# Attention outputs in one fp32 piece, returns on GpSimd's queue, and another order of filler and finishing in a fused attention layer

## The chip, the cores and the metric

The kernel runs on one core of a Trainium2 chip. The metric is the device time of one launch in microseconds (us). The time before is the median of three runs. One further execution was recorded by the hardware profiler; all rows of a profile are from that execution.

## The reference

One decoder layer on 512 tokens of width 2048, in fp32: native sparse attention with 16 heads of 128 in 4 groups, then a SwiGLU feed-forward block, RMS norms before both and at the end. Cut to what matters here:

```python
hn = rmsnorm(x, mix_norm_g)
q, kc, vc, ks, vs, kw, vw, gl = split(hn @ w_in)        # 16 q heads; 4 groups of keys and values
p_c = masked_softmax(q @ kcc + bias_c)                  # compressed branch: 31 blocks per group
p_s = masked_softmax(q @ ks + bias)                     # selected branch: 16 blocks wanted, 8 exist, so all
p_w = masked_softmax(q @ kw + bias)                     # window of 512: all tokens before
o   = g0 * (p_c @ vcc) + g1 * (p_s @ vs) + g2 * (p_w @ vw)   # per head, gates g = sigmoid(gl)
h   = x + o.reshape(S, 2048) @ w_out
out = rmsnorm(h + (silu(a) * b) @ ffn_w_out, final_norm_g)   # a, b = rmsnorm(h) @ ffn_w_in
```

## The kernel before

fp32 products are made of three TensorE matmuls. Each operand is split into a high part of a shorter type (fp32r), made by a copy on ScalarE, and a low part, made by a subtraction on VectorE; `three()` (L266 to 269) adds high x high, high x low and low x high. Weights arrive by DMA as `raw` in pieces of 128x1024, and `Weights.split` makes `whi` (ScalarE, L97) and `wlo` (VectorE, L98) of each, some pieces ahead of their use. In the attention stage the weights' loads go on GpSimd's queue. Each engine runs its instructions in the order in which the program emits them; a DMA that must wait also holds what stands behind it on its queue.

The attention stage lies at about 200 to 700 us of the profiled execution. Sixteen heads follow each other, each in twelve steps. For head h and step i the loop emits, in this order:

- `fetch(t)` (L812): the probabilities of the 128 tokens of tile t are read back from DRAM (`d_p`) into `ptr`, in another order. It is on SyncE's queue.
- `turn`: one piece of the probabilities is split into `pth` (ScalarE, L829) and `ptl` (VectorE, L833; the compressed branch's piece in L831). Steps 0 to 8.
- `scores(h+1, t)` at steps 2, 5, 8 and 11 for t = 3, 2, 1, 0: matmuls of q and k, then on VectorE a sum with the bias and its maximum (L791, `mx`), and on ScalarE the exponential (L793), into a buffer `P[t]`. Tiles 3 and 1 share one buffer, tiles 2 and 0 the other.
- `finish(h+1, t)` at steps 3, 6 and 9 for t = 3, 2, 1, and at step 0 of the head itself for t = 0: VectorE normalizes and gates the probabilities (L798 to 805) and turns them in blocks of 32x32 (L806); four DMAs on SyncE's queue write them to `d_p` (L808).
- `values`: the matmuls of probabilities and v (`o`), from step 2 on, two steps behind their `turn`. The last of a head, at step 10, is the compressed branch's (L844, with `vcc`). Then `head_out` (L849) splits the head's output: heads 12 to 15 straight into `hn_h` and `hn_l`, heads 0 to 11 into two tiles `of`, which two DMAs write to DRAM (`d_o`).
- `pump` (L735): filler from one long generator, `dense()`, whose granules are 3 matmuls of 512 columns or 6 of 256 and count 650 ns in the program's own accounts. The filler makes q of two heads, then the keys or the values of a group, in units of 32 granules (q, k, q, v, q, k, ...: thirteen units, the last one q of heads 14 and 15, written q14 below), and then four `partial` products of the output projection, of 24 granules each. `pump` emits until the accounts reach a goal that grows with head and step: four steps ahead, at 20,800 ns a head up to the thirteenth unit and 18,300 from there on. A q unit ends in an eviction: `yt` (VectorE, L319), `qh` (ScalarE, L292), `ql` (VectorE, L293).

`hn_h` and `hn_l` first hold the normed input that the filler multiplies. While q14 is emitted, the outputs of heads 0 to 11 come back from `d_o` into these tiles (`reload_o`, six DMAs of 1 MB on SyncE's queue, each after the matmuls that used that part). A partial product (L699) multiplies heads 0 to 11 with a quarter of the columns that it covers, adds x, which a DMA on SyncE's queue brings into `stage`, and a DMA on that queue writes the sum to `d_h`.

Ahead of the loop a prologue emits the scores (0,3) to (0,0) of head 0 with some filler behind each (`pump(-1, ...)`), and their `finish` and `fetch`. Behind the loop come the rest of the output projection and the feed-forward block, to the end of the span.

Of the kernel before, what the change touches and what calls it, by code (L numbers as in the profile page):

```python
# [10 lines left out]
F32 = mybir.dt.float32  # L11
F32R = mybir.dt.float32r
I32 = mybir.dt.int32
AF = mybir.ActivationFunctionType
OP = mybir.AluOpType
# [4 lines left out]
S, D, H, DH, G, HPG = 512, 2048, 16, 128, 4, 4  # L20
# [153 lines left out]
def nsa_block(ctx: ExitStack, tc: tile.TileContext, x, rel_bias, mix_g, ffn_g, fin_g, w_in, w_out,  # L174
              pos_k, w1k, w2k, pos_v, w1v, w2v, f_in, f_out, onehot, out):
    nc = tc.nc
    mm, act, dve, pool = nc.tensor.matmul, nc.scalar.activation, nc.vector, nc.gpsimd
# [6 lines left out]
    dram = ctx.enter_context(tc.tile_pool(name="dram", bufs=1, space=DRAM))  # L184
# [10 lines left out]
    hn_h, hn_l = hn_t = [hnp.tile([128, KC, S], F32R, name=f"hn_{x}") for x in "hl"]  # L195
    d_t = dram.tile([H, UL], F32, name="d_t")
    d_u = dram.tile([128, H * UL], F32, name="d_u")
    d_c = dram.tile([H, 16 * CL], F32, name="d_c")
    d_o = dram.tile([12, 2, 128, S], F32, name="d_o")
    d_h = dram.tile([S, 256 * N_SPILL], F32, name="d_h")  # L200
    d_r = dram.tile([NT, 128, D], F32, name="d_r")
    d_a = dram.tile([NF // 2, 128, 2 * S], F32, name="d_a")
# [87 lines left out]
    def split_from(psum_ap, hi, lo, scale=None):  # L290
        if scale is None:
            act(hi, psum_ap, AF.Copy)  # L292
            dve.tensor_tensor(lo, psum_ap, hi.bitcast(F32), op=OP.subtract)  # L293
        else:
            act(hi, psum_ap, AF.Copy, scale=scale)
            dve.scalar_tensor_tensor(lo, psum_ap, scale, hi.bitcast(F32), op0=OP.mult, op1=OP.subtract)
# [333 lines left out]
    with ExitStack() as st2:  # L630
# [24 lines left out]
        def qpair(h0):  # L655
            ps = proj2()
            end = q_out(ps, h0)
            for i in range(4):
                yield from ws(ps, i, W.take(), end=end)
                if h0 == H - 2 and i < 3:  # L660
                    reload_o(i)
            done["n"] += 1
            yield None

# [27 lines left out]
            yield None  # L692

        def reload_o(i):
            for part, t in enumerate((hn_h, hn_l)):
                nc.sync.dma_start(t[:, 4 * i:4 * i + 4].bitcast(F32),
                                  d_o[4 * i:4 * i + 4, part].rearrange("h p s -> p h s"))

        def partial(cb):  # L699
            st = stage_tile().rearrange("p (t c) -> p t c", t=NT)  # L700
            c = slice(256 * cb, 256 * (cb + 1))
            nc.sync.dma_start(st, x[:, c].rearrange("(t p) c -> p t c", p=128))
            ps = [p.rearrange("p (t c) -> p t c", t=2) for p in proj2()]
            for i in range(3):
                w = W.take()
                for t in range(NT):
                    if i == 2 and t == 2:
                        W.ahead(3)
                    for k in range(4):
                        h = 4 * i + k  # L710
                        three(ps[t // 2][:, t % 2], hn_h[:, h, tok(t)], hn_l[:, h, tok(t)], w[0][:, k], w[1][:, k],
                              h == 0 and t % 2 == 0, h == 11)
                        if k % 2:
                            yield 650
                    if i == 2 and t % 2:
                        b = t // 2
                        dve.tensor_tensor(st[:, 2 * b:2 * b + 2], st[:, 2 * b:2 * b + 2], ps[b], op=OP.add)
            nc.sync.dma_start(d_h[:, c].rearrange("(t p) c -> p t c", p=128), st)
            done["n"] += 1
            yield None  # L720

# [12 lines left out]
        STEPS = 12  # L734

        def pump(h, step):
            at = h + (step + 4) / STEPS
            goal = 20800 * min(at, 13) + 18300 * max(at - 13, 0)
            while done["ns"] < goal:
                c = next(stream, "end")  # L740
                if c == "end":
                    return
                done["ns"] += c or 0
# [66 lines left out]
        def fetch(t):  # L810

            nc.sync.dma_start(PT[:, :, PT_STEP * t:PT_STEP * t + runs[t]], d_p[t].rearrange("j a i r -> (j a) i r"))  # L812
# [6 lines left out]
        def turn(h, b, kt):  # L819
            n = S - 128 * kt  # L820
            th = ap_.tile([128, 512], F32R, name="pth", bufs=3)
            tl = ap_.tile([128, 512], F32R, name="ptl")
            rows = 128 if b >= 0 else 96
            if b < 0:
                src = arrived(rows, 64, 0, PT_STEP + 64)
            else:
                src = arrived(rows, PT_STEP * kt + 32 * (kt + 1) * b + 32 * kt, kt, PT_STEP + 32 * b)
            th4, tl4 = (x[:rows, :n].rearrange("p (t i s) -> p t i s", i=4, s=32) for x in (th, tl))
            act(th4, src, AF.Copy)  # L829
            if b < 0:  # L830
                dve.tensor_tensor(th4[32:64], src[32:64], th4[32:64].bitcast(F32), op=OP.subtract)  # L831
            else:
                dve.tensor_tensor(tl4, src, th4.bitcast(F32), op=OP.subtract)  # L833
            HS[h]["t", b, kt] = th[:rows, :n], tl[:rows, :n]
# [14 lines left out]
        def head_out(h):  # L849
            o = HS[h]["o"]  # L850
            if h < 12:
                f = [ap_.tile([128, S], F32R, name=f"of{i}", bufs=1) for i in range(2)]
                split_from(o, *f)
                for i in range(2):
                    nc.sync.dma_start(d_o[h, i], f[i].bitcast(F32))
            else:
                split_from(o, hn_h[:, h], hn_l[:, h])
            del HS[h]
# [2 lines left out]
        load_bias(0)  # L861
        load_bias(1)
        for i in range(4):
            scores(0, 3 - i)
            if i:
                finish(0, 4 - i)
            if i > 1:
                fetch(5 - i)
            pump(-1, min(9 + i, 11.7))
        for h in range(H):  # L870
            seq = [(b, kt) for kt in (3, 2, 1, 0) for b in (0, 1)] + [(-1, 0)]
            for i in range(STEPS):
                if i == 4:
                    load_bias(h + 2)
                if i in (0, 3):
                    fetch(1 - i // 3)
                if i < 9:
                    turn(h, *seq[i])
                if i == 8 and h + 1 < H:
                    fetch(3)  # L880
                    fetch(2)
                if i == 0:
                    finish(h, 0)
                if h + 1 < H:
                    if i == 2:
                        drain_to(needed(h + 1))
                    if i % 3 == 2:
                        scores(h + 1, 3 - i // 3)
                    elif i % 3 == 0 and i:
                        finish(h + 1, 4 - i // 3)  # L890
                if 2 <= i < 11:
                    if i == 2 and h % HPG == 0:
                        drain_to(h)
                    values(h, *seq[i - 2])
                    if i == 10:
                        head_out(h)
                pump(h, i)
        W.queue = nc.sync
# [591 lines left out]
```

## Time and profile before

| | |
|---|---|
| median of three runs | 2136.5 us (2135.11 to 2139.32) |
| the profiled execution | 2137.68 us, of which its span is 2136.0 us |
| attention stage | about 200 to 700 us |
| TensorE busy | 2103.2 us, 98% of the span |
| VectorE busy | 1634.8 us, 77% |
| ScalarE busy | 922.9 us, 43% |
| granted TensorE clock, mean | 0.996 |

In the profile PE is TensorE, PEld its weight load, DVE VectorE, ACT ScalarE, POOL GpSimd, SP SyncE, and SPq a DMA queue fed by SyncE. A row of a timeline gives start, duration, engine, line, operation, output and inputs, partitions and elements, and in brackets the engine's idle time before it and what ended it. A row of the busy times by stretch gives, for each engine, the busy us and the instructions in it, then the granted clock (PEclk), the busy share of the DMA engines and their GB/s. A row of the waits gives the engine and line that waited, what released it, the us in total, the times and the longest.

### The profile page before, as it was taken

The numbers are of one execution on the slowest core, as the hardware profiler recorded it, in microseconds if no ns is written. First come the engines' busy times: TensorE is split into PE (matmuls) and PEld (weight loads), VectorE is DVE, ScalarE is ACT, GpSimd is POOL, SyncE is SP. The second block draws the span as 40 slices with busy tenths as digits, with TensorE's granted clock in tenths as the row PEclk, the third lists the DMA queues.
The fourth block names the chain that finished last, engine by engine and source line by source line (L and its number), as shares of the span: only waits on it lengthen the run. The fifth ranks groups of instructions, "written<-read, shape, count | busy, mean of one in ns | idle before, by whom it ended". The sixth has DMA issues, their size and how long they took to land.

```text
span 2136.0 us, 37198 instructions
## 1 busy us (share of the span) xinstructions
PE 2103.2 (98%) x14697; PEld 1949.5 (91%) x14697; DVE 1634.8 (77%) x2680; ACT 922.9 (43%) x1433; POOL 118.2 (6%) x195
## 2 busy tenths in 40 slices
PE   9999999999998999999999999999999999999998
PEld 7898788898988889899999999999999888999996
DVE  5565777878776357898888888888888787877785
ACT  5344454555544234444444343443434444544344
POOL 1000111111100000000000000000000000001000
PEclk9999999999999999999999999999999999999999
DMA  7555777776787643344434344433344776878894
GB/s 226 174 158 149 195 203 202 194 209 197 207 295 211 218 137 111 118 130 128 129 126 122 122 126 129 129 119 125 123 129 129 256 278 220 299 268 308 307 336 143
DMA packets 279147, 394.37 MB, mean 185 GB/s; under 512 B 34763, under 2 KB 208891, under 8 KB 278332
## 3 DMA queue, kind: packets, MB, share of 16 engines
q1 hardware_dynamic: 255324, 289.68, 43.5%
q0 software_dynamic: 21744, 98.12, 13.3%
q10 hardware_dynamic: 1904, 4.20, 0.5%
q8 instruction: 115, 1.88, 0.4%
q14 instruction: 60, 0.49, 0.1%
HBM read 323.67 MB, written 73.50 MB: 186 GB/s over the span
## 4 chain that ended last, share of the span: by engine, by line
PE 87%; DVE 5%; DMA 4%; ACT 2%; issue 2%; SPq 1%; POOL 0%; ACTq 0%; DVEq 0%; POOLq 0%
PE f L268 19%; PE f L269 19%; PE f L267 19%; PE proj L267 7%; PE proj L268 6%; PE proj L269 6%; DMA d_p<-p 1%; DVE wlo L98 1%; DMA ptr<-d_p 1%; PE pp L269 1%; PE pp L268 1%; PE pp L267 1%; PE po L269 1%; PE po L267 1%; PE po L268 1%
## 5 line engine op out<-in xcount | busy, mean ns | idle before, releaser
L98 DVE TENSOR_TENSOR wlo<-raw,whi 128x1024 fp32r<-128x1024 f32 (+1 forms) x226 | 270.6, 1200 | 117.2 <-ACT whi L97 116.7
L97 ACT ACTIVATE whi<-raw 128x1024 fp32r<-128x1024 f32 (+1 forms) x226 | 234.4, 1040 | 230.4 <-DVE raw L989 124.7
L989 DVE TENSOR_TENSOR tlo<-tt,thi 128x1536 fp32r<-128x1536 f32 (+2 forms) x135 | 197.1, 1460 | 110.1 <-ACT thi L1091 89.1
L267 PE MATMUL f<-hn_h,whi 128*128 128x256 f32 x984 | 271.7, 276 | 0.8 <-ACT E L1049 0.8
L269 PE MATMUL f<-hn_h,wlo 128*128 128x256 f32 x984 | 271.6, 276 | 0.0
L268 PE MATMUL f<-hn_l,whi 128*128 128x256 f32 x984 | 271.6, 276 | 0.0
L1086 ACT ACTIVATE whi<-raw 128x1024 fp32r<-128x1024 f32 x123 | 126.1, 1057 | 292.2 <-DVE raw L989 281.9
L267 PE MATMUL proj<-hn_h,whi 128*128 128x512 f32 x512 | 204.1, 399 | 0.5 <-ACT hn_h L402 0.5
L268 PE MATMUL proj<-hn_l,whi 128*128 128x512 f32 x512 | 200.7, 392 | 0.3 <-DVE hn_l L403 0.3
L269 PE MATMUL proj<-hn_h,wlo 128*128 128x512 f32 x512 | 200.9, 392 | 0.0
L267 PEld LDWEIGHTS f<-hn_h,whi 128*128 128x128 f32 x984 | 184.7, 188 | 1.2 <-ACT E L1049 1.2
L269 PEld LDWEIGHTS f<-hn_h,wlo 128*128 128x128 f32 x984 | 184.7, 188 | 0.0
L268 PEld LDWEIGHTS f<-hn_l,whi 128*128 128x128 f32 x984 | 184.7, 188 | 0.0
L1091 ACT ACTIVATE thi<-tt 128x1536 fp32r<-128x1536 f32 x82 | 121.8, 1486 | 84.8 <-PE f L268 75.3
L989 DVE TENSOR_TENSOR wlo<-raw,whi 128x1024 fp32r<-128x1024 f32 x123 | 147.0, 1223 | 0.0
L267 PE MATMUL proj<-whi,hn_h 128*128 128x256 f32 (+2 forms) x496 | 146.7, 296 | 0.0
L269 PE MATMUL proj<-whi,hn_l 128*128 128x256 f32 (+2 forms) x496 | 146.0, 294 | 0.0
L268 PE MATMUL proj<-wlo,hn_h 128*128 128x256 f32 (+2 forms) x496 | 145.9, 294 | 0.0
L269 PE MATMUL f<-whi,tlo 128*128 128x512 f32 x320 | 124.9, 390 | 0.6 <-DVE tlo L989 0.6
L268 PE MATMUL f<-wlo,thi 128*128 128x512 f32 x320 | 125.0, 391 | 0.0
L267 PE MATMUL f<-whi,thi 128*128 128x512 f32 x320 | 124.7, 390 | 0.0
L269 PEld LDWEIGHTS proj<-hn_h,wlo 128*128 128x128 f32 x512 | 96.5, 189 | 21.5 <-DVE wlo L98 0.2
(323 smaller groups left out, 6087.1 us busy)
## 6 DMA issues: line engine op xcount, KB each, us to landing
raw<-in_ffn_w_in SPq DMA_DIRECT2D x135, 512.0 KB, 3.8
raw<-in_ffn_w_out SPq DMA_DIRECT2D x88, 512.0 KB, 5.7
rawx<-in_ffn_w_in SPq DMA_DIRECT2D x41, 512.0 KB, 4.8
rawx<-d_a SPq DMA_DIRECT2D x31, 512.0 KB, 5.2
ah<-d_s POOLq DMA_DIRECT2D x16, 896.0 KB, 7.0
al<-d_s POOLq DMA_DIRECT2D x16, 896.0 KB, 9.5
raw<-in_nsa_w_in SPq DMA_DIRECT2D x24, 512.0 KB, 5.1
raw<-in_nsa_w_in POOLq DMA_DIRECT2D x24, 512.0 KB, 4.7
```

Source lines behind the costliest of these rows:

```text
L97: self.nc.scalar.activation(hi[:, :n], src, AF.Copy)
L98: self.nc.vector.tensor_tensor(lo[:, :n], src, hi[:, :n].bitcast(F32), op=OP.subtract)
L267: mm(o, ah, bh, start=start, stop=False, skip_group_check=True)
L268: mm(o, ah, bl, start=False, stop=False, skip_group_check=True)
L269: mm(o, al, bh, start=False, stop=stop, skip_group_check=True)
L989: dve.tensor_tensor(o, a, b, op=OP.subtract)
L1086: act(h, r, AF.Copy)
L1091: act(h, ttf, AF.Copy)
```

## The change

- `d_o` holds one fp32 piece per head. `head_out` of heads 0 to 11 is a copy on ScalarE and one DMA. `reload_o` brings three pieces of 1 MB into `hn_l`, on GpSimd's queue, and a new function `split_o` splits two heads at a time: a copy into `hn_h` on ScalarE and a subtraction in place on VectorE. Two of its six calls are emitted in q14, behind the granules of its third and fourth piece of weights, four in the first partial product, ahead of the matmuls of its first two pieces.
- The x loads of the partial products and the writes to `d_h` go on GpSimd's queue, and the load is emitted at the second piece of weights.
- `pump` runs eight steps ahead, and from the thirteenth unit on at 20,400 ns a head. In the prologue it is called ahead of each of the four scores, with goals of 6, 7.5, 9 and 10.5 steps, and once behind them.
- `finish(h+1, t)` for t = 3, 2, 1 stands at steps 5, 8 and 11, behind that step's scores. `fetch(1)` moves from step 0 to 1, `fetch(2)` from 8 to 10. The last `values` of a head and `head_out` move from step 10 to 11. `ptl` has three buffers in place of two.

```diff
--- before.py
+++ after.py
@@ -196,7 +196,7 @@
     d_t = dram.tile([H, UL], F32, name="d_t")
     d_u = dram.tile([128, H * UL], F32, name="d_u")
     d_c = dram.tile([H, 16 * CL], F32, name="d_c")
-    d_o = dram.tile([12, 2, 128, S], F32, name="d_o")
+    d_o = dram.tile([12, 128, S], F32, name="d_o")
     d_h = dram.tile([S, 256 * N_SPILL], F32, name="d_h")
     d_r = dram.tile([NT, 128, D], F32, name="d_r")
     d_a = dram.tile([NF // 2, 128, 2 * S], F32, name="d_a")
@@ -659,6 +659,8 @@
                 yield from ws(ps, i, W.take(), end=end)
                 if h0 == H - 2 and i < 3:
                     reload_o(i)
+                if h0 == H - 2 and i > 1:
+                    split_o(i - 2)
             done["n"] += 1
             yield None
 
@@ -692,18 +694,24 @@
             yield None
 
         def reload_o(i):
-            for part, t in enumerate((hn_h, hn_l)):
-                nc.sync.dma_start(t[:, 4 * i:4 * i + 4].bitcast(F32),
-                                  d_o[4 * i:4 * i + 4, part].rearrange("h p s -> p h s"))
+            pool.dma_start(hn_l[:, 4 * i:4 * i + 4].bitcast(F32), d_o[4 * i:4 * i + 4].rearrange("h p s -> p h s"))
+
+        def split_o(k):
+            h, l = (x[:, 2 * k:2 * k + 2] for x in (hn_h, hn_l))
+            act(h, l.bitcast(F32), AF.Copy)
+            dve.tensor_tensor(l, l.bitcast(F32), h.bitcast(F32), op=OP.subtract)
 
         def partial(cb):
             st = stage_tile().rearrange("p (t c) -> p t c", t=NT)
             c = slice(256 * cb, 256 * (cb + 1))
-            nc.sync.dma_start(st, x[:, c].rearrange("(t p) c -> p t c", p=128))
             ps = [p.rearrange("p (t c) -> p t c", t=2) for p in proj2()]
             for i in range(3):
                 w = W.take()
+                if i == 1:
+                    pool.dma_start(st, x[:, c].rearrange("(t p) c -> p t c", p=128))
                 for t in range(NT):
+                    if not cb and i < 2 and t % 2 == 0:
+                        split_o(2 + 2 * i + t // 2)
                     if i == 2 and t == 2:
                         W.ahead(3)
                     for k in range(4):
@@ -715,7 +723,7 @@
                     if i == 2 and t % 2:
                         b = t // 2
                         dve.tensor_tensor(st[:, 2 * b:2 * b + 2], st[:, 2 * b:2 * b + 2], ps[b], op=OP.add)
-            nc.sync.dma_start(d_h[:, c].rearrange("(t p) c -> p t c", p=128), st)
+            pool.dma_start(d_h[:, c].rearrange("(t p) c -> p t c", p=128), st)
             done["n"] += 1
             yield None
 
@@ -734,8 +742,8 @@
         STEPS = 12
 
         def pump(h, step):
-            at = h + (step + 4) / STEPS
-            goal = 20800 * min(at, 13) + 18300 * max(at - 13, 0)
+            at = h + (step + 8) / STEPS
+            goal = 20800 * min(at, 13) + 20400 * max(at - 13, 0)
             while done["ns"] < goal:
                 c = next(stream, "end")
                 if c == "end":
@@ -819,7 +827,7 @@
         def turn(h, b, kt):
             n = S - 128 * kt
             th = ap_.tile([128, 512], F32R, name="pth", bufs=3)
-            tl = ap_.tile([128, 512], F32R, name="ptl")
+            tl = ap_.tile([128, 512], F32R, name="ptl", bufs=3)
             rows = 128 if b >= 0 else 96
             if b < 0:
                 src = arrived(rows, 64, 0, PT_STEP + 64)
@@ -849,10 +857,9 @@
         def head_out(h):
             o = HS[h]["o"]
             if h < 12:
-                f = [ap_.tile([128, S], F32R, name=f"of{i}", bufs=1) for i in range(2)]
-                split_from(o, *f)
-                for i in range(2):
-                    nc.sync.dma_start(d_o[h, i], f[i].bitcast(F32))
+                f = ap_.tile([128, S], F32, name="of", bufs=1)
+                act(f, o, AF.Copy)
+                nc.sync.dma_start(d_o[h], f)
             else:
                 split_from(o, hn_h[:, h], hn_l[:, h])
             del HS[h]
@@ -861,23 +868,25 @@
         load_bias(0)
         load_bias(1)
         for i in range(4):
+            pump(-1, 6 + 1.5 * i)
             scores(0, 3 - i)
             if i:
                 finish(0, 4 - i)
             if i > 1:
                 fetch(5 - i)
-            pump(-1, min(9 + i, 11.7))
+        pump(-1, 11.7)
         for h in range(H):
             seq = [(b, kt) for kt in (3, 2, 1, 0) for b in (0, 1)] + [(-1, 0)]
             for i in range(STEPS):
                 if i == 4:
                     load_bias(h + 2)
-                if i in (0, 3):
+                if i in (1, 3):
                     fetch(1 - i // 3)
                 if i < 9:
                     turn(h, *seq[i])
                 if i == 8 and h + 1 < H:
                     fetch(3)
+                if i == 10 and h + 1 < H:
                     fetch(2)
                 if i == 0:
                     finish(h, 0)
@@ -886,13 +895,13 @@
                         drain_to(needed(h + 1))
                     if i % 3 == 2:
                         scores(h + 1, 3 - i // 3)
-                    elif i % 3 == 0 and i:
-                        finish(h + 1, 4 - i // 3)
-                if 2 <= i < 11:
+                        if i > 2:
+                            finish(h + 1, 4 - i // 3)
+                if 2 <= i < 10 or i == 11:
                     if i == 2 and h % HPG == 0:
                         drain_to(h)
-                    values(h, *seq[i - 2])
-                    if i == 10:
+                    values(h, *seq[min(i - 2, 8)])
+                    if i == 11:
                         head_out(h)
                 pump(h, i)
         W.queue = nc.sync
```

## The prediction

> **What bounds the kernel now.** I read the page first, then the busy time by stretch, the waits of TensorE, its timeline around each wait, and the queues behind them.
>
> ```profile
> span 2136.0 us, 37198 instructions
> PE 2103.2 (98%) x14697; PEld 1949.5 (91%) x14697; DVE 1634.8 (77%) x2680; ACT 922.9 (43%) x1433; POOL 118.2 (6%) x195
> ```
>
> TensorE is busy 98% of the span, and no matmul is removed. So the change can only win or lose TensorE's idle time, and what the clock loses after it. The diff touches the attention stage alone, 200 to 700 us. By stretch (busy us, PEclk the granted clock as a share of full speed):
>
> ```profile
> 200.00:250.00 50.00, 43.23 (x200) 35.02 (x199) 36.25 (x105) 22.63 (x61) 4.50 (x6) 0.97 0.62 168
> 250.00:600.00 350.00, 348.21 (x1980) 304.91 (x1979) 276.44 (x768) 178.91 (x480) 49.28 (x66) 1.00 0.73 207
> 600.00:700.00 100.00, 90.41 (x664) 85.35 (x663) 67.68 (x181) 40.80 (x106) 8.85 (x12) 0.97 0.75 238
> 235.00:240.00 5.00, 5.00 (x17) 4.08 (x16) 3.47 (x11) 3.53 (x9) 0.54 (x1) 0.67 0.73 224
> 620.00:625.00 5.00, 4.99 (x27) 4.85 (x28) 4.75 (x16) 2.49 (x7) 0.75 (x1) 0.66 0.62 183
> 690.00:695.00 5.00, 4.46 (x22) 4.21 (x23) 1.78 (x4) 2.16 (x5) 0.00 (x0) 0.72 0.47 144
> ```
>
> Idle is 50−43.23 = 6.8 us in head 0, 350−348.21 = 1.8 in heads 1 to 12, 100−90.41 = 9.6 after, 18.2 in all. Three stretches of 5 us ran at 0.67, 0.66 and 0.72: they lost 1.65, 1.7 and 1.4 us, 4.75 together. About 23 us can be won at most. Who ended the idle (us in total, times, longest):
>
> ```profile
> PE o L267 <- ACT pth L829: 5.6, 3, 2.7
> PE o L268 <- DVE ptl L833: 4.1, 2, 2.3
> PE o L844 <- DVE pth L831: 2.6, 5, 1.3
> PE o L267 <- issue: 2.5, 1, 2.5
> PE s L267 <- DVE yt L319: 1.7, 1, 1.7
> PE s L267 <- DVE mx L791: 0.7, 1, 0.7
> ```
>
> ```profile
> 234.26 0.44 PE L268 MATMUL o<-ptl,v0h 128*128 128x384 f32 x1 [1.84 <-DVE ptl L833]
> ...
> 306.58 0.50 PE L844 MATMUL o<-pth,vcc 96*128 96x512 f32 x1 [0.23 <-DVE pth L831]
> ...
> 366.77 0.50 PE L844 MATMUL o<-pth,vcc 96*128 96x512 f32 x1 [0.37 <-DVE pth L831]
> ...
> 620.01 0.33 PE L267 MATMUL o<-pth,v1h 128*128 128x128 f32 x1 [2.73 <-ACT pth L829]
> ...
> 690.39 0.44 PE L267 MATMUL o<-pth,v1h 128*128 128x384 f32 x1 [1.83 <-ACT pth L829]
> ```
>
> Two heads take 366.77−306.58 = 60.2, so a head takes 30.1 us and a step 2.5. The middle has hardly a gap; the losses are at the two ends. What decides is whether the ends get cheaper without the middle becoming tight.
>
> **Prologue and head 0.** The prologue emits 24 granules of filler before the scores (0,1), not 14. Ten more, at the program's own 0.65 us each, are 6.5 us, and they lie where TensorE waited 1.7 (yt) and 0.7 (mx). These 2.4 us go. The waits of 2.5 (issue) and 1.8 (ptl) follow from the probabilities' way through DRAM, which is not shortened:
>
> ```profile
> 216.62 0.51 ACT L793 ACTIVATE p<-u,mx 128x256 f32<-128x256 f32 x1 [3.64 <-DMA d_p<-p]
> ```
>
> Tiles 3 and 1 (2 and 0) share a buffer, so ScalarE stood 3.64 us in front of the exponentials of (0,1) until the writes of tile 3 had landed. In the new order the weight splits and the eviction of the next q stand on ScalarE and VectorE behind such a wait. Ends: 4.3 us of idle with the old half clock of 1.65, 6; with two more waits of 3.64 seen by TensorE and a second half clock, 15. I take the middle, 10.5, against 8.4 now: **+2.1**.
>
> **Heads 1 to 11.** The saving: twelve outputs lose their VectorE subtraction, 0.66 us each by its row, 8 us in all. VectorE is busy 276 of 350, and idle before ptl 46.8, so this is off the path. The cost: finish moves from steps 3, 6, 9 to 5, 8, 11, behind the new scores, while the tile that reuses its buffer stays at step 8 or 11. The distance shrinks from five steps to three, 7.5 us. Rows of five views, in this order: VectorE's timeline (two), SyncE's queue, the DMA issues (median us to landing last), VectorE's waits and its groups in 250 to 600:
>
> ```profile
> 208.48 0.19 DVE L791 CUSTOM_DVE_ANT_0 cx<-s,biasc 128x31 f32<-128x31 f32 x1 [1.59 <-PE s L269]
> ...
> 212.44 0.08 DVE L791 DVE_READ_ACCUMULATOR2_ANT mx<- 128x1 f32 x1
> 492.29 2.61 SPq L808 DMA_DIRECT2D d_p<-p  x4
> d_p<-p SPq DMA_DIRECT2D x64, 144.0 KB, 2.6
> DVE ptl L833 <- ACT pth L829: 46.8, 36, 2.6
> L293 DVE TENSOR_TENSOR of<-o,of 128x512 fp32r<-128x512 f32 x12 | 7.9, 662 | 0.0
> ```
>
> Scores and finish of one step take VectorE 212.44−208.48 = 4.0 us, then the four writes take 2.6 to issue and 2.6 to land: 9.2 against 7.5. So the exponentials wait about 1.7 us, twice a head; behind them on ScalarE stand pth and the weights' whi, behind those on VectorE ptl and wlo, and for wlo TensorE has no substitute. VectorE's idle before ptl, 46.8/11.6 heads = 4 us a head, can absorb 3.4. Ends: 0, where it does; 1.3 a head in the nine heads whose filler is q or k, 12, where the wait comes on top of VectorE's own queue. I take 0.4 per such head plus 1.4 of today's 1.8: 5 against 1.8, **+3.2**. The filler runs eight steps ahead instead of four, so a unit's last granules, and its eviction, now fall at step 4, not 8: its yt, ql and wlo meet the finish of step 5. That is why I do not take zero.
>
> **Heads 12 to 14.** Today's loss is 1.3 (vcc), 2.73, 1.0, 2.3 and the half clock of 1.7, about 9.
>
> ```profile
> 616.00 0.49 SPq L702 DMA_DIRECT2D stage<-in_x  x1
> 621.87 0.53 SPq L812 DMA_DIRECT2D ptr<-d_p  x1
> hn_l<-d_o SPq DMA_DIRECT2D x3, 1024.0 KB, 10.1
> ```
>
> SyncE's queue holds the reloads (six of 1 MB, 10 us to land) and the x loads between the probabilities' fetches. Now three pieces of 1 MB go on GpSimd's queue, the x loads too, and SyncE is free: I take all these gaps as gone but 0.5. Behind a waiting reload on GpSimd stand the weight loads only; they run ahead of their use, so I price it at 0, at most 3 if a weight comes late. The reload needs hn_l's old contents used up, as today.
>
> [...] The order on SyncE speaks for a saving.
>
> In their place comes a new wait. fp32 pieces must be split again: six split_o, a ScalarE copy and a VectorE subtraction of 128x1024. Two follow in unit q14, four in the first partial. By the instruction order the partial does only 6 matmuls before it needs the heads of split_o(1), whose subtraction stands on VectorE behind the scores (13,2) and finish (13,3).
>
> ```profile
> L98 DVE TENSOR_TENSOR wlo<-raw,whi 128x1024 fp32r<-128x1024 f32 (+1 forms) x226 | 270.6, 1200 | 117.2 <-ACT whi L97 116.7
> 481.85 0.28 PE L269 MATMUL s<-k0h,ql 128*128 128x256 f32 x1
> 487.28 0.19 DVE L791 CUSTOM_DVE_ANT_0 cx<-s,biasc 128x31 f32<-128x31 f32 x1
> ```
>
> Lower end: scores and finish 4.0, the subtraction 1.2 (the row of the same shape), less about 1.1 of TensorE work between (6 matmuls and a value): 4.1. Upper end: VectorE starts a step's scores late, at 487.28 after matmuls that ended at 482.13, 5.15 us: 9.3. The latter row is a q eviction meeting scores, which is this place; I take 7.5, and a half clock of 1.7 behind it. With 0.5 left in heads 13 and 14: 9.7 against 9, **+0.7**.
>
> [...]
>
> **Head 15.** The rate of the filler after unit 13 rises, and it runs ahead: the four partials are 62,400 of the program's ns, of which 18,300×2.25 = 41,200 were asked for by the end of head 14 and 20,400×2.58 = 52,700 now are. So 9,700 are left for head 15 against 21,200, and the filler ends at step 5, not 12. The rows are from SyncE's queue and ScalarE's timeline.
>
> ```profile
> 676.82 2.08 SPq L808 DMA_DIRECT2D d_p<-p  x4
> 689.81 0.94 ACT L829 ACTIVATE pth<-ptr 128x384 fp32r<-128x384 f32 x2 [7.28 <-DMA ptr<-d_p]
> ```
>
> From the writes of tile 1 to its pth are 13.0 us. Now its finish stands behind the last scores, some 3 us: 16 us after these scores. TensorE has the filler and four values to do meanwhile, about 10 + 3.9: it waits 2.1, or 5.2 with a VectorE backlog of 3; I take 3.3 and 1 for a likely half clock: 4.3 against 1.8+1.4 = 3.2, but a shorter tail of x and d_h transfers on SyncE may give some back: **+0.6**.
>
> **Sum.** 2.1+3.2+0.7+0.6 = +6.6: 2143.1 on the median of 2136.5; on the profiled execution (2137.68: the span of 2136.0 and 1.7 around it, 1.2 above the median) 2144.3.
>
> **Rivals.** *Faster, 2128.* SyncE's relief removes the gaps of heads 12 to 14 (9), the loop stays free (0 instead of +3.2) as VectorE's 4 us of idle a head absorb the wait, head 0 gains 2.4, and the split costs its lower end, 4.1, without half clock; head 15 stays: −9+4.1−2.4 = −7.3, and up to −9 with a better head 15. It decides if writes land within about 7.5 us of the scores. For it speaks the near-gapless middle; against it the late VectorE at 487.28. *Much slower, 2152.* The exponentials' wait is seen in every q or k head: 12 instead of 5, and head 0 goes to 13: +6.6+7+2.5 = +16. It decides when the writes land in over 5.2 us. Against it: the 46.8 us before ptl. *No change, 2137.* Head 0 gains 2.4, the middle loses 2, the rest balances. Not doing what it says is possible for one part: the cover of eight steps could be used up by the waiting weights.
>
> **How the numbers follow.** A measurement tells about 0.2%, 4.3 us, from no change. Chances: forecast 0.42, faster rival 0.29, no change 0.17, much slower 0.12. The forecast's own range is 2140 to 2148, and the whole range 2127 to 2154 reaches into both rivals. The faster rival and an edge of no change give 0.30 for faster; 0.18 the same; the rest, 0.52, is slower.
>
> **What would show it.** Right: a gap of 4 to 9 us on the second group of matmuls of the first partial, ended by split_o's subtraction, and a half clock after it; gaps on wlo at the start of units in heads 1 to 11, ended by whi behind p; the gap at 620.01 gone; a gap of 2 to 5 us in head 15 on pth. Wrong: heads still of 30.1 us, the wait before ptl still some 4 us a head, the first partial without a gap. A head of over 31 us shows the much slower rival.

## The result, and the profile after

The changed kernel takes 2169.7 us (median of four runs, 2167.5 to 2170.4) against 2136.4: a ratio of 1.0153, 95% interval 1.0139 to 1.0166. It is slower by 33 us. The forecast was 2143, its range 2127 to 2154: the sign was right, the size was not, and the range missed.

The head of the page of the changed kernel:

```profile
span 2168.0 us, 37134 instructions
PE 2112.3 (97%) x14697; PEld 1953.7 (90%) x14697; DVE 1637.1 (76%) x2674; ACT 933.4 (43%) x1439; POOL 127.2 (6%) x207
```

The span grew by 32.0 us, with the same number of matmuls. Busy times by stretch, columns as before (lines have moved too: L841 is the L833 of the kernel before, L837 its L829):

```profile
200.00:250.00 50.00, 42.27 (x197) 33.73 (x197) 32.37 (x90) 20.50 (x54) 4.50 (x6) 1.00 0.53 146
250.00:600.00 350.00, 335.10 (x1889) 290.92 (x1889) 259.48 (x724) 173.02 (x454) 48.57 (x65) 1.00 0.64 184
600.00:700.00 100.00, 86.40 (x585) 80.22 (x584) 68.71 (x178) 45.56 (x112) 13.52 (x18) 0.91 0.66 201
700.00:750.00 50.00, 43.97 (x278) 39.72 (x278) 28.35 (x65) 18.81 (x41) 5.82 (x8) 0.93 0.71 231
```

TensorE's idle from 200 to 750 us is 550-507.7 = 42.3 us, against 18.2 in the kernel before: +24. By the granted clock 0.09x100+0.07x50 = 12.5 us are lost, but nearly 4 of them lie in waits (of the 13.65 us at half clock from 628.42 on TensorE was busy for 6.21); the trace leaves 8.2 us, against 5.1 before (three half clocks of 1.7): +3. The remaining 5 us of the 32 stand in the trace as busy time: the next matmul starts 0.23 us (the median) after one of 512 columns, whose own row has 0.39 us, so it counts 0.23 where another follows it and its whole 0.39 where TensorE runs dry behind it, and that happens 43 times, against 23 before. By place: the middle (250 to 600) lost 14.9 us where it had lost 1.8; the heads from 12 on (600 to 750) lost 19.6 us of idle and 8.2 of clock where it had been 9.6 and 3.4. Who ended the idle from 200 to 750 us:

```profile
PE o L268 <- DVE ptl L841: 23.5, 30, 1.3
PE proj L267 <- ACT hn_h L701: 8.1, 1, 8.1
PE o L267 <- ACT pth L837: 6.7, 6, 2.3
PE s L267 <- DVE sm L806: 2.3, 1, 2.3
PE proj L269 <- DVE hn_l L702: 1.3, 1, 1.3
```

Thirty waits on `ptl`, of up to 1.3 us, are the new thing: about two a head, and 14.7 of the 14.9 us in the middle are theirs. One of them, in head 5, in TensorE's timeline and then in VectorE's and ScalarE's:

```profile
405.03 0.50 PE L268 MATMUL o<-ptl,v1h 128*128 128x512 f32 x1 [1.25 <-DVE ptl L841]
```

```profile
399.37 0.69 DVE L293 TENSOR_TENSOR k0l<-yt,k0h 128x512 fp32r<-128x512 f32 x1 [0.70 <-ACT k0h L292]
399.98 0.55 DVE L841 TENSOR_TENSOR ptl<-ptr,pth 128x384 fp32r<-128x384 f32 x1
400.45 0.18 DVE L799 CUSTOM_DVE_ANT_0 cx<-s,biasc 128x31 f32<-128x31 f32 x1
...
403.02 1.38 DVE L814 STREAM_TRANSPOSE p<-p 128x1152 f32<-128x1152 f32 x1
404.32 1.25 DVE L841 TENSOR_TENSOR ptl<-ptr,pth 128x512 fp32r<-128x512 f32 x2
```

```profile
402.61 1.66 ACT L837 ACTIVATE pth<-ptr 128x512 fp32r<-128x512 f32 x3
```

VectorE finishes the eviction of a key (`k0l`), then the scores of step 5 from 400.45, then the moved `finish` (to 404.3), and only then the `ptl` of steps 6 and 7. TensorE had already begun that product and stood still in the middle of it. The eviction and the `finish` stand together ahead of the `ptl`; the trace does not say which of the two is to blame. The experiments had to.

The other new thing is in head 12:

```profile
634.56 0.58 PE L267 MATMUL proj<-whi,hn_h 128*128 128x256 f32 x1 [8.08 <-ACT hn_h L701]
...
636.66 0.58 PE L269 MATMUL proj<-whi,hn_l 128*128 128x256 f32 x1 [1.30 <-DVE hn_l L702]
```

```profile
600.00:650.00 50.00, 37.26 (x191) 32.24 (x190) 31.11 (x74) 22.95 (x51) 4.55 (x6) 0.83 0.59 187
616.00:620.00 4.00, 4.00 (x16) 3.23 (x16) 1.50 (x8) 0.83 (x3) 0.00 (x0) 0.73 0.97 327
628.00:632.00 4.00, 0.00 (x0) 0.00 (x0) 3.30 (x8) 1.27 (x3) 0.75 (x1) 0.55 0.61 224
632.00:636.00 4.00, 0.80 (x2) 0.50 (x2) 3.90 (x11) 3.94 (x10) 0.00 (x0) 0.50 0.03 10
636.00:640.00 4.00, 3.34 (x14) 3.34 (x15) 3.47 (x4) 0.92 (x1) 0.00 (x0) 0.50 0.64 153
```

The first partial product waits 8.1 us for the split of heads 2 and 3 and 1.3 for its low part. The clock drops to half at 628.4, 1.9 us into the wait, and stays there until 642.0. ScalarE came to the copy of these heads late, behind the last eviction of q14 and the exponentials of the scores (13,2):

```profile
633.46 1.99 ACT L701 ACTIVATE hn_h<-hn_l 128x1024 fp32r<-128x1024 f32 x2
```

### The profile page after: what moved, and what is told of

Read it like the earlier page. It is cut to its first block, busy times and chain, and to the rows that moved or that the text cites. A ratio compares the mean times of both kernels' runs of the same rounds, so it can differ in the third digit from the quotient of the medians.

```text
span 2168.0 us, 37134 instructions
## 1 busy us (share of the span) xinstructions
PE 2112.3 (97%) x14697; PEld 1953.7 (90%) x14697; DVE 1637.1 (76%) x2674; ACT 933.4 (43%) x1439; POOL 127.2 (6%) x207
## 4 chain that ended last, share of the span: by engine, by line
PE 82%; DVE 6%; DMA 5%; ACT 3%; issue 2%; SPq 1%; ACTq 0%; DVEq 0%
PE f L268 19%; PE f L269 19%; PE f L267 19%; PE proj L267 5%; PE proj L269 5%; PE proj L268 5%; DMA d_p<-p 3%; DMA ptr<-d_p 1%; ACT whi L97 1%; DVE ptl L841 1%; SPq L816 1%; DVE p L813 1%; PE pp L269 1%; PE pp L268 1%; PE pp L267 1%
```

## The experiments

Each was timed with runs of the kernel before on the same chip (2135.2 to 2136.8 us). Medians, ratio to the kernel before with its interval, and the mean length of heads 1 to 10 from one compressed product (`vcc`) to the next in the profile:

| run | us | ratio | head, us |
|---|---|---|---|
| before | 2136.4 | | 30.1 |
| changed | 2169.7 | 1.0153 [1.0139, 1.0166] | 31.8 |
| a_fin: finish early | 2197.9 | 1.0286 [1.0271, 1.0302] | 34.3 |
| a_old: finish and fetches early | 2182.3 | 1.0216 [1.0202, 1.0230] | 33.4 |
| a_four: four ahead | 2139.2 | 1.0010 [1.0001, 1.0020] | 30.3 |
| a_finfour: four ahead, finish early | 2156.3 | 1.0092 [1.0077, 1.0107] | 31.8 |
| a_two: two pieces | 2156.4 | 1.0091 [1.0076, 1.0106] | 31.9 |
| a_two4: two pieces, four ahead | 2144.1 | 1.0030 [1.0018, 1.0042] | 31.0 |
| a_two13: two pieces, thirteen ahead | 2146.1 | 1.0042 [1.0028, 1.0057] | 30.2 |
| a4s: four ahead, early splits | 2135.9 | 0.9998 [0.9989, 1.0007] | 30.6 |
| a4sp: and the old prologue | 2135.7 | 0.9997 [0.9988, 1.0006] | 30.4 |
| a1s: one ahead, early splits | 2134.1 | 0.9990 [0.9981, 0.9998] | 29.9 |
| b_eight: before, eight ahead | 2185.1 | 1.0235 [1.0220, 1.0251] | 33.5 |
| b_fetch: before, late fetches | 2160.4 | 1.0111 [1.0096, 1.0126] | 32.0 |
| b_fin: before, late fetches and finish | 2155.7 | 1.0089 [1.0073, 1.0106] | 30.9 |
| b_pool: before, GpSimd's queue | 2139.9 | 1.0034 [1.0020, 1.0047] | 30.1 |
| best | 2130.1 | 0.9976 [0.9967, 0.9985] | 29.8 |

### Finish or eviction

a_fin undoes the place of `finish`, a_four the lead of the filler, a_finfour both:

```diff
-                        if i > 2:
-                            finish(h + 1, 4 - i // 3)
+                    elif i % 3 == 0 and i:
+                        finish(h + 1, 4 - i // 3)
```

```diff
-            at = h + (step + 8) / STEPS
+            at = h + (step + 4) / STEPS
```

> The changed kernel with one part undone: finish(h+1, 3/2/1) back at steps 3, 6 and 9, everything else as changed. Theory ORDER (the lines of finish stand on VectorE ahead of the ptl that the values of the same head need, so TensorE waits 1.2 us in the middle of a product, head after head): the waits of TensorE on ptl fall from 23.5 us to under 10, heads 1 to 11 return to 30.1 to 30.4 us, the gap in head 12 loses about 4 of its 8 us: 2150 to 2155. Rival EVICTION (the q and k evictions, now at steps 4 and 5 and not 8 and 9, meet the scores of step 5 on VectorE): the loop stays near 31.5 us a head, 2165. If both are needed: 2150 here and in the run with the filler four steps ahead.

> The changed kernel with the filler four steps ahead again (in the prologue too, four steps less at each call), finish behind the scores as changed. EVICTION: heads 1 to 11 return to 30.1 to 30.4 us, the gap of head 12 shrinks to 4 us or less as the eviction of q14 moves away from the split of the outputs: about 2152. ORDER: the loop stays at 31 us or more a head, the waits on ptl over 15 us; 2160 to 2168, less only by what head 15 regains.

> Both undone: finish at steps 3, 6, 9 and the filler four steps ahead; left are the fp32 pieces with their splits, the transfers on GpSimd's queue, the shifted fetches and last values, three ptl buffers and the higher rate. All theories: the loop is as before, 30.1 us a head. What is left over 2136.5 is then the price of the splits in head 12 and of heads 12 to 15: 2138 to 2146; below 2136.5 would mean that the freed SyncE queue pays.

My first theory, ORDER, fell: with `finish` early again the kernel is 28 us slower still, not 15 faster (a_old, below, shows the same with the fetches taken back too). Taking back four of the eight steps gives 30.5 us: 7.7 us of idle go in the middle, 10.0 from 600 to 750, the rest is clock and matmuls in front of waits. So the lead of the filler is the price, and the late `finish` is a gain in its company. EVICTION had the heads right (30.3 us) but not the size: it gave 2152, and a gap in head 12 of 4 us or less, which stayed at 6.8. And a_finfour, at 2156, was not the 2138 to 2146 that every theory had given: something else went with `finish`. Two runs asked what.

### The fetches

b_fetch moves the fetches alone in the kernel before; b_fin moves `finish` with them.

```diff
-                if i in (0, 3):
+                if i in (1, 3):
                     fetch(1 - i // 3)
...
-                    fetch(2)
+                if i == 10 and h + 1 < H:
+                    fetch(2)
```

> The kernel before with the fetches alone moved as in the change: fetch(1) from step 0 to 1, so that it stands behind finish(0)'s four writes on SyncE's queue, and fetch(2) from step 8 to 10. Finish stays at steps 3, 6, 9. Theory FETCH (undoing finish alone cost 17 us in the run four steps ahead because the fetches stayed late for an early finish): heads of 31 us and more with waits on ptl of 128x384, 2148 to 2154. Rival (the early finish itself is what costs there): 2137.

> The kernel before with finish at steps 5, 8, 11 behind the scores and the fetches at steps 1, 3, 8, 10 as in the change; the rest is as before. If finish behind the scores is a gain by itself: 2128 to 2134, with the gaps before vcc gone. If it only fits the later fetches: 2137. The prediction's term said +3.

FETCH held and was too small, 24 us against 12 to 18, and the fetch that costs is not the one that I had named. SyncE's queue and ScalarE between heads 2 and 3 of b_fetch:

```profile
315.13 3.40 SPq L808 DMA_DIRECT2D d_p<-p  x4
318.64 0.52 SPq L812 DMA_DIRECT2D ptr<-d_p  x1
```

```profile
323.08 0.42 ACT L829 ACTIVATE pth<-ptr 128x256 fp32r<-128x256 f32 x1 [4.77 <-DMA ptr<-d_p]
```

`fetch(2)`, at step 10, stands behind the writes of tile 1, which step 9 emitted and which wait for VectorE until 315.13. It is issued at 318.64; in the kernel before the two fetches of step 8 went out at 306.56, in a loop that was 3.6 us ahead. ScalarE then waits 4.8 us for tile 2, with everything behind it. The change moved `finish(1)` from step 9 to 11, so `fetch(2)` at step 10 stands ahead of it again: the two moves fit together. `finish` undone alone is a loss (a_fin, a_finfour), and so is the move of the fetches alone; a changed kernel with the fetches alone undone was not run.

In b_fin neither case held. The loop takes 30.9 us a head, 0.8 over the kernel before, and the rest of its 19 us is lost in heads 12 to 15, where TensorE waits 7.6 us for a fetch that SyncE issued at 597.48, right behind two returns, and that took 12.0 us to land. So late `finish` and fetches together, without the rest of the change, cost the loop about 8 us over ten heads. In a_four the head is down to 30.3; of the parts that it has besides, a_two4 below points to the one fp32 piece, since without it the head takes 31.0 again. Three `ptl` buffers and the last values at step 11 were not tried alone.

a_old asks the question of `finish` or eviction without that confusion: `finish` and fetches both where they were, the filler eight ahead.

> The changed kernel (eight steps ahead) with finish at steps 3, 6, 9 and both fetches at steps 0 and 8 as before; all else as changed. It asks whether the eviction at step 4 costs by itself or only together with the finish at step 5. PLACE alone (a q or k eviction in the stretch where turn needs VectorE is enough): heads of 31 us and more, 2158 to 2166. BOTH (finish and eviction must meet on step 5): heads of 30.1 to 30.5 us, 2148 to 2152, the rest being the gap of head 12.

> The kernel before with one part alone: the filler eight steps ahead instead of four. PLACE (the q, k and v evictions, now at steps 4 and 5, stand on VectorE and ScalarE ahead of what the values need): heads of 31.5 to 33.5 us, as in the run with the early finish and fetches, and 2155 to 2180. Rival (the loss needs the later finish or the splits): 2137 to 2145.

Heads of 33.4 us: eviction and `finish` need not meet on step 5. The time, 2182, lies 16 us above what PLACE had given. b_eight, the kernel before with nothing changed but the 4 that became an 8, loses 50 us, with 20.5 us of idle in the middle. Its rows, VectorE's, ScalarE's and TensorE's in head 4:

```profile
377.64 1.38 DVE L806 STREAM_TRANSPOSE p<-p 128x1152 f32<-128x1152 f32 x1
378.94 0.65 DVE L319 SCALAR_TENSOR_TENSOR yt<-proj,ybc 128x512 f32<-128x512 f32 x1
...
381.23 1.23 DVE L98 TENSOR_TENSOR wlo<-raw,whi 128x1024 fp32r<-128x1024 f32 x1 [0.26 <-ACT whi L97]
382.38 0.55 DVE L833 TENSOR_TENSOR ptl<-ptr,pth 128x384 fp32r<-128x384 f32 x1
```

```profile
379.62 0.63 ACT L292 ACTIVATE qh<-yt 128x512 fp32r<-128x512 f32 x1 [4.78 <-DVE yt L319]
380.16 1.04 ACT L97 ACTIVATE whi<-raw 128x1024 fp32r<-128x1024 f32 x1
381.11 0.51 ACT L829 ACTIVATE pth<-ptr 128x384 fp32r<-128x384 f32 x1
```

```profile
381.67 0.45 PE L267 MATMUL o<-pth,v1h 128*128 128x384 f32 x1 [1.84 <-ACT pth L829]
382.98 0.46 PE L268 MATMUL o<-ptl,v1h 128*128 128x384 f32 x1 [0.87 <-DVE ptl L833]
```

This is the mechanism where `finish` is early. The unit of filler ends at step 4, in the stretch in which the values need a `turn` at every step. Its `yt` stands on VectorE behind `finish`; its `qh` waits 4.8 us for `yt` at the head of ScalarE's line, and the `pth` that the values need stands behind `qh`, its `ptl` behind `ql` and `wlo`. TensorE waits for both. At step 8 the last `turn` of a head is issued; there the same chain holds up little (a_four, 30.3 us a head). The middle of b_eight and of a_four:

```profile
250.00:600.00 350.00, 329.54 (x1762) 283.52 (x1761) 254.25 (x692) 161.28 (x428) 46.95 (x61) 0.96 0.63 179
```

```profile
250.00:600.00 350.00, 342.78 (x1950) 300.55 (x1949) 266.10 (x739) 181.14 (x473) 50.88 (x68) 1.00 0.68 194
```

20.5 us of idle and 4% of the clock in the one, 7.2 and none in the other.

### Place or lead

If the place of the eviction is the cause, a lead of thirteen steps must be harmless, since it puts the eviction at step 11. The run is in two pieces (below), with the lead held at the twelfth unit:

```diff
             at = h + (step + 8) / STEPS
+            at = max(at, min(at + 5 / STEPS, 12))
```

> As the run in two pieces, but the filler thirteen steps ahead (held at the twelfth unit until eight steps ahead reach it, since the returns of the last heads must not be asked for before they are written). A unit then ends, and its eviction falls, at step 11 of a head, as it would with one step ahead; in the changed kernel at step 4, before at step 8. Theory PLACE (what costs is the eviction at step 4, in the stretch where the values need ptl; any place behind step 8 is free): heads 1 to 9 take 29.7 to 30.3 us, no matter how far ahead. Rival LEAD (running far ahead costs by itself: buffers of q, k, v come free late and the weights' splits crowd): heads of 31.5 us or more. The hold in head 11 may cost up to 8 us, so the total is read second: 2126 to 2140 against 2156 or more.

Heads 1 to 9 take 30.2 us on average, against 31.8 with eight ahead. PLACE holds, LEAD falls: further ahead is no worse. The total, 2146, is 6 us over my range: the hold leaves idle in heads 11 and 12, and head 15 another 4.3 us.

### The split of the fp32 pieces, and the queue

a_two keeps eight steps ahead and makes the outputs in two pieces again, which go to DRAM from the tile `stage`; the six returns are on GpSimd's queue. a_two4 is the same four steps ahead.

```diff
-                f = ap_.tile([128, S], F32, name="of", bufs=1)
-                act(f, o, AF.Copy)
-                nc.sync.dma_start(d_o[h], f)
+                st = stage_tile().bitcast(F32R)
+                f = [st[:, 512 * i:512 * i + 512] for i in range(2)]
+                split_from(o, *f)
+                for i in range(2):
+                    nc.sync.dma_start(d_o[h, i], f[i].bitcast(F32))
```

> The changed kernel with the outputs of twelve heads in two pieces, split when they are made as before (six returns of 1 MB, on GpSimd's queue, no split_o). Theory SPLIT (the 8 us gap in the first partial product and the half clock behind it come from the new splits standing behind exponentials on ScalarE and behind scores and finish on VectorE): the gap goes and with it 10 to 14 us: 2156 to 2160, with the loop as in the changed kernel. Rival TRAFFIC (the gap is due to a fetch that took 7.7 us under the returns' traffic, and all else follows): twice the bytes make it no better, 2168 or more.

> The changed kernel with two things undone: the filler four steps ahead, and the outputs in two pieces (returns still on GpSimd's queue). If the two prices add (eight steps ahead 30.5 us, the split of fp32 pieces 13.3 us): 2169.7-30.5-13.3 = 2126, faster than the kernel before by 0.5%, as TensorE's idle in head 12 goes and the rest of the change (finish behind the scores, prologue, SyncE's queue) is kept. If they overlap, because the gap in head 12 was in part the eviction's: 2130 to 2136.

The first fits SPLIT: the gap is gone and 13.3 us with it (no wait of TensorE from 600 to 650 is over 1 us). The second does not: 2144, not 2126, and slower than a_four with its gap of 6.8. Its waits show what took the place of the gap:

```profile
PE o L268 <- DVE ptl L839: 10.8, 14, 1.2
PE o L267 <- ACT pth L835: 6.2, 3, 5.2
PE o L267 <- DVE stage L293: 2.0, 2, 1.1
```

One wait of 5.2 us on `pth` comes while the six returns run (a fetch issued at 598.52 took 9.3 us to land); the waits on `ptl` are 10.8 against 5.6 in a_four; and twice a head's first value waits for the subtraction that reads the one PSUM tile `o` (2.0), a wait that a_four does not have. The prediction had priced this side of the fp32 piece at nothing. b_pool tests the queue alone:

```diff
-                nc.sync.dma_start(t[:, 4 * i:4 * i + 4].bitcast(F32),
+                pool.dma_start(t[:, 4 * i:4 * i + 4].bitcast(F32),
...
-            nc.sync.dma_start(st, x[:, c].rearrange("(t p) c -> p t c", p=128))
+            pool.dma_start(st, x[:, c].rearrange("(t p) c -> p t c", p=128))
```

> The kernel before with one part alone: the returns (still six of 1 MB), the x loads and the writes to d_h on GpSimd's queue. Theory ORDER ON SYNCE (the probabilities' fetches stood behind waiting returns and loads): the gaps of 2.7, 1.0, 2.3 and 1.8 us in heads 12 to 15 go, with the two half clocks 8 to 10 us less: 2127 to 2129. Rival TRAFFIC (the fetches are slow since 16 DMA engines are full, whoever issues): 2134 to 2138, the gap near 620 still there.

It is 4.8 us slower, not 8 to 10 faster. SyncE's queue, ScalarE and the busy times by stretch in head 12 of the profiled execution (which took 2147.2 us):

```profile
592.09 0.53 SPq L812 DMA_DIRECT2D ptr<-d_p  x1
```

```profile
601.10 0.94 ACT L829 ACTIVATE pth<-ptr 128x384 fp32r<-128x384 f32 x2 [6.20 <-DMA ptr<-d_p]
```

```profile
595.00:600.00 5.00, 1.76 (x10) 1.16 (x8) 3.29 (x5) 0.00 (x0) 1.01 (x2) 1.00 1.04 392
```

SyncE issued the fetch at once, and it took 9.0 us to land: the DMA engines' busy share was 1.04 from 595 to 600, at 392 GB/s, with returns that GpSimd had issued. TRAFFIC holds, with a time 2 us above its range. The trace of the kernel before had shown it already: the two fetches that SyncE issued from 608.77 on, ahead of the gap at 620.01, were not held on the queue but landed late, under the last two returns (issued at 604.98 and 605.95). The issues from 608 to 612 us, the median to landing last:

```profile
ptr<-d_p SPq DMA_DIRECT2D x1, 576.0 KB, 10.8
ptr<-d_p SPq DMA_DIRECT2D x1, 448.0 KB, 9.8
```

608.77+10.8 is 619.6, where that gap ends. So SyncE's order was not what made it. Why b_pool is slower than the kernel before, and not level with it, was not settled; its trace has two waits on `pth` in head 12, of 4.9 and 3.5 us, each behind a fetch that ran under returns.

### Toward a better version

Three runs put both `split_o` calls of q14 behind its third piece of weights. a4s and a4sp run four steps ahead, a4sp with the old prologue, a1s one step.

```diff
-                if h0 == H - 2 and i > 1:
-                    split_o(i - 2)
+                if h0 == H - 2 and i == 2:
+                    split_o(0)
+                    split_o(1)
```

> The changed kernel with the filler four steps ahead, and split_o(0) and split_o(1) both behind the third piece of weights of q14 instead of behind the third and the fourth, 8 granules earlier. If the gap of 6.8 us ahead of the first partial product is only the late place of split_o(1): it falls to under 1.5 us and the half clock behind it goes, 2139.2-7 to 2139.2-9 = 2130 to 2132. If the gap is replaced by one at the split of heads 4 to 7, or by a wait for the returns on ScalarE: 2136 to 2139.

> As the run with four steps ahead and the earlier splits, but one step ahead, so that an eviction falls at step 11. PLACE: heads as with four or thirteen steps ahead, 29.7 to 30.3 us, 2127 to 2134. LEAD would give the same or better here. Against it: TensorE's filler at the start of head 0 is shorter by three steps, which may leave 2 to 4 us of gaps there: then 2131 to 2136.

> As the run with four steps ahead and the earlier splits, with the prologue's filler behind the scores as in the kernel before (calls of 9, 10, 11 and 11.7 steps). In the kernel before with finish alone moved, head 0 ended 3.5 us earlier than in the kernel before and in the run with four steps ahead. If the spread prologue costs at four steps ahead: 3 us under the run beside it, 2127 to 2129. If it gains, as the term of the prediction has it for two gaps of 2.4 us: 2 us over it.

The gap ahead of the first partial product, in a_four and in a4s:

```profile
616.82 0.58 PE L267 MATMUL proj<-whi,hn_h 128*128 128x256 f32 x1 [6.83 <-ACT hn_h L701]
```

```profile
619.36 0.38 PE L267 MATMUL proj<-whi,hn_h 128*128 128x256 f32 x1 [2.17 <-ACT hn_h L702]
```

It falls from 6.8 us to 2.2, but only 3.3 us of the total go, where 7 to 9 were expected: the mean granted clock of the profiled execution only rose from 0.995 to 0.996, a wait of 2.0 on a fetch under the returns is there, and the next head is longer (34.6 us against 29.4). a4s and a4sp differ by 0.2 us, so the spread prologue is worth nothing that can be seen at four steps ahead; I had expected 3 us one way or 2 the other. One step ahead gives the quietest loop of all, as its stretches show, and pays for it in head 0, where no filler is left between the scores:

```profile
200.00:250.00 50.00, 42.39 (x186) 34.15 (x185) 35.14 (x106) 22.25 (x63) 4.26 (x6) 0.90 0.60 165
250.00:600.00 350.00, 349.76 (x1988) 307.59 (x1987) 274.06 (x763) 184.53 (x483) 51.60 (x69) 1.00 0.69 198
```

The last run lets the lead fall from four steps to one:

```diff
-            at = h + (step + 8) / STEPS
+            at = h + (step + max(1, 4 - max(h + step / STEPS, 0))) / STEPS
```

> The changed kernel with the filler's lead falling from four steps in head 0 to one step from head 3 on, the prologue's filler as in the kernel before, and split_o(0) and split_o(1) both behind q14's third piece. PLACE: the loop's heads at 29.7 to 30.3 us as with one step ahead (idle under 1 us in 250 to 600), head 0 as in the run with the old prologue (idle 5 us, no half clock) and not the 7.6 and a half clock of the run one step ahead: 2134-2.7-5 = 2126, and 2130 if part of it is lost in heads 1 to 3, where the lead changes.

```profile
200.00:250.00 50.00, 45.05 (x215) 36.60 (x214) 37.67 (x111) 24.33 (x70) 4.52 (x6) 1.00 0.63 177
250.00:600.00 350.00, 348.36 (x1971) 304.77 (x1971) 273.20 (x763) 183.88 (x480) 52.16 (x69) 1.00 0.70 199
600.00:700.00 100.00, 94.25 (x714) 89.84 (x713) 72.09 (x175) 46.70 (x108) 14.86 (x20) 0.98 0.68 208
```

2130.1 us against 2135.2 in the same comparison, ratio 0.9976 [0.9967, 0.9985]: faster than the kernel before by 5.1 us, and so than both. Head 0 keeps the idle of 5 us without a half clock; 1.6 us are lost in the middle, where the lead changes (waits of 0.8 and 0.4 near 267 and 281), and 5.8 from 600 on. The longest wait there, 2.0 us on `pth` at 612.26, is the old cost again, in ScalarE's rows:

```profile
611.38 0.63 ACT L292 ACTIVATE qh<-yt 128x512 fp32r<-128x512 f32 x1 [1.36 <-DVE yt L319]
611.92 0.29 ACT L838 ACTIVATE pth<-ptr 128x128 fp32r<-128x128 f32 x1
```

The last eviction of q14 waits for `yt`, and the `pth` of head 13's first values stands behind it.

## Why the prediction was right or wrong

**Head 0, +2.1.** Too high, and with the sign turned. Idle from 200 to 250 us went from 6.8 to 7.7, but the half clock of 1.7 there is gone (1.00 against 0.97): about -0.8. The waits of 1.7 and 0.7 went as forecast, and so did that of 2.5; in their place stand 2.3 on `sm` and 5.2 on `pth` and `ptl`. (Ahead of the scores (0,1) the new goals ask for 14 granules against 6: eight more, not the ten of the prediction.)

**Heads 1 to 11, +3.2.** The step that failed. Measured: 14.9 us of idle in 250 to 600 against 1.8, +13.1, over even the upper end of +10. The prediction saw that the evictions move to step 4, spent two sentences on it and gave it no price of its own; it priced the exponentials' wait for the writes instead. That wait came, and near its size. From 250 to 600 us of the changed kernel:

```profile
ACT p L801 <- DMA d_p<-p: 34.2, 17, 3.2
DVE wlo L98 <- ACT whi L97: 61.8, 43, 3.6
PE o L268 <- DVE ptl L841: 14.7, 19, 1.3
```

Seventeen waits of 2.0 us on average, against 1.7 twice a head in the forecast. But they are not what TensorE pays for: b_eight and a_old have none of them from 250 to 600 and lose more there (20.5 and 18.2 us of idle), and a_four keeps 23.9 us of them with 7.2 of idle. Nor does TensorE wait on `wlo`, where I had looked: it waits on `ptl`, behind the eviction. b_eight prices the lead alone at 50 us. And the cover that the term relied on, VectorE's idle of 4 us a head before `ptl`, was a mean over the head: behind the eviction, from 399.4 to 405.6, VectorE has no pause. In the changed kernel this idle is down from 46.8 to 0.2 us; VectorE stands before `wlo` instead.

**Finish behind the scores.** As a cost of about 3 it was near what a_four shows without the lead: idle in 250 to 600 of 7.2 us (350-342.8), 5.4 more than before. With the eight steps it is part of a gain: a_old to the changed kernel, -12.7 us for `finish` and fetches together.

**Heads 12 to 14, +0.7.** The gap in the first partial product was forecast in its place, at 7.5 us in a range to 9.3; 8.1+1.3 = 9.4 were measured. What ended it was not the subtraction on VectorE, as forecast, but the copy on ScalarE, behind q14's eviction and the exponentials; the subtraction added the 1.3. The half clock was mis-sized: 1.7 was allowed, and from 600 to 650 it cost 4.8 us while TensorE was busy, since it held until 642.0 and an earlier one had followed two shorter gaps (0.73 at 616, after gaps of 1.33 and 0.93). All other gaps were put at 0.5; 13.6-9.4 = 4.2 us of idle remain beside it. The step "I take all these gaps as gone" was wrong in its reason, as b_pool and the fetches of 10.8 and 9.8 us in the kernel before show: the saving by SyncE's order, which it relied on, was not there. With the returns issued by GpSimd, b_pool's fetch, issued at once, still took 9.0 us to land.

**Head 15, +0.6.** Right in kind: waits on `pth` of 2.3 and 1.1 at 722 and 734, and on `ptl` behind both. Too small: 6.0 us of idle and 3.4 of clock in 700 to 750, against 1.8 and 1.4 before.

**The sign and the rivals.** The forecast said slower and it is slower, but through a cost that the sum did not hold, so the sign is in good part luck. The much slower rival (2152) named the loop as what binds, at 12 us, and the loop lost 14.9, but for another reason; the rest of the 33 came from heads 12 to 15. No case held an eviction as its mechanism.

## What to carry to other kernels

How far ahead filler runs is two numbers: how much is in hand, and where in the cycle its unit ends. The second can be worth more: choose the lead so that a unit's eviction falls in the stretch in which the critical chain needs neither of the engines that it uses (here the last steps of a head), whether the lead is small or large (one step and thirteen steps of a cycle of twelve end the unit at the same place). Price a moved instruction by walking the queue of every engine that it touches (in b_eight's row `qh` waited 4.8 us on ScalarE, with `whi` and the `pth` behind it), and the operand behind it that the bound engine needs next; and do not undo one of two moves that were made for each other and call the result the price of one.

## What the runs showed of the hardware that was not expected

- A half clock of 3.41 us began at 614.76 in the changed kernel (0.73 over 616 to 620), behind gaps of only 1.33 and 0.93 us with a few matmuls between. The seven gaps of 1.24 to 1.34 us from 250 to 600 were followed by none (1.00 over that stretch, with 14.9 us of idle); in b_eight, with ten pairs of 0.58 to 1.84 and about 0.87 us, the same stretch ran at 0.96.
- The length of a gap did not tell which is followed by a half clock. In the kernel before half clocks of 3.41 us began at 234.84, 620.55 and 692.23, behind gaps of 1.84, 2.73 and 1.83 us, while the gaps of 2.51 us (to 222.32) and 2.26 us (to 663.29) were followed by none: 1.00 from 222 to 228 and from 663 to 670. What decides it was not settled, so the price of a gap could not be read from its length.
- A fetch of 320 KB, issued without delay, took 9.0 us to land while the DMA engines moved 392 GB/s (b_pool); the median of this size in the attention stage of the kernel before was 3.4 us.
